# A two-layer retention and attention trunk in float32: the retention heads issued in another order, kept tiles reloaded by GpSimd, weight sums moved by 192 bytes

## The chip, the core and the metric

The kernel runs on one core of one Trainium2 chip. The metric is the device time of one execution in microseconds (us), given as the median of several runs. The profile is of one execution; its times are counted from the start of the span. Engines in the profile: PE is TensorE (PEld its weight loads), DVE is VectorE, ACT is ScalarE, POOL is GpSimd, SP is SyncE. SP does nothing but issue DMAs, and here GpSimd does little else.

## The reference

Two layers, 512 tokens, model width 1024, everything float32. A layer is a half-step SwiGLU FFN, a token mixer, another half-step FFN and a gated per-layer embedding, with an RMS norm ahead of each; the mixer of layer 0 is retention, that of layer 1 is forgetting attention. Each FFN is `h = h + 0.5 * swiglu(rmsnorm(h), w_in, w_out)` with 2816 hidden features. The part that the change touches most is retention, four heads with 256 features for q and k and 512 for v:

```python
def retention(h, w_in, gn_w, w_out):
    q, k, v, g = jnp.split(h @ w_in, ...)
    q = rotary(q); k = rotary(k) * DK ** -0.5
    # per head, causal, with a decay gamma ** (i - j) between tokens i >= j
    s = (q @ k.T) * decay
    o = rmsnorm(s @ v, gn_w)        # per head
    y = silu(g) * o
    return y @ w_out
```

The reference works in chunks of 128 tokens and carries a state. The kernel computes the same as one causal product over the 512 tokens.

## The kernel before, in words

**Products.** A float32 product is made of three TensorE products of rounded halves (`mm3`, L339 to L341): every operand is split into a high part `hi` (a rounding copy, `nc.scalar.copy`, on ScalarE: L329) and a low part `lo` (the operand minus `hi`, on VectorE: L330). Activations live as pairs of 128x512 tiles in four pools, `unit_a` to `unit_d`. Weights come through `Weights`: SP loads a raw tile (L80), ScalarE and VectorE split it (L88, L89); where `negated` is used, ScalarE writes the high part and the negated raw tile (L134, L135) and GpSimd adds the source on top with an accumulating DMA (L136). For the first two heads of retention all output weights (`ret_o`) take this second way.

**Strassen.** The FFNs' input products and retention's projections of q, k and gates are computed in pairs with seven half-size products instead of eight (`Strassen`, its products in `product`, L540). They need sums of weight blocks, `s12`, `s34` and the split block `a12`, which `emit_sums_now` makes on VectorE (L168) and splits, in a pool that is opened per stage (`ffn0` to `ffn3`, and `rsum` for retention). A product of L540 has 128x128 weights from such a tile, and a half-width unit tile (128x256) as the moving operand. By the compiled program's addresses, all unit tiles start at 32 modulo 512 bytes; `s12`, `s34` and `a12` start at 224 modulo 512 in the FFN stages and at 288 in retention; raw weight splits `w8` start at 32 or at 224.

**Retention's stage.** First all projections: v (L525), then 14 Strassen pairs for q, k and gates of the heads. q and k are rotated, gates go through silu, and everything that head 0 doesn't need at once is written to 28 tiles in DRAM (`kept`) by GpSimd DMAs (L798, L824). Then the heads, one after the other:

- `loaded(hd)` reloads q, k and v of a head: eight DMAs of 256 KB into unit tiles (only the four of v for head 0; L832, issued by SP), each followed by a rounding copy on ScalarE (L833) and a subtraction on VectorE (L834).
- `scores(hd)` multiplies q by k (PE), scales by the decay (L889, VectorE) and splits the result into `uhi0..3` and `ulo0..3`; these are the u of the change's title.
- `attended` multiplies u by v into four banks and squares them (L910).
- `head_scale` sums the squares over tokens (L353), `on_rows` brings the scale to rows (L490 transposes, L929).
- `kept_gates(hd)` reloads the gates (`sg`, L945, SP); for head 0 they are computed late (`gate`, L937).
- `outputs(hd)` scales the four banks (L952), multiplies by the gates (L956) and splits into `unit_a` tiles, d = 0 to 3.
- `out_blocks` multiplies former outputs by `ret_o`, one block of 128 output features at a time, and adds to the residual `hall` (L971).

**What sets the order.** TensorE runs the program in the order in which it is written (`manual_schedule`). ScalarE, VectorE, GpSimd and SP are ordered by the scheduler that compiles the kernel, which starts from the program's text and from `issue_after`, which keeps an instruction behind another. Each engine then works strictly in that order: an instruction that waits holds up all that stand behind it on its engine. A DMA that GpSimd issues stands in GpSimd's DMA queue, one that SP issues in another.

**FFN.** `ffn` runs the first two or three hidden blocks plainly (`plain`), because the norm's scale isn't there yet, and the rest as Strassen pairs: `begin` starts a pair's products, `rest` does the others, `next_sums` lets VectorE make the sums of the next. The `columns` and `rows` of the norm bring the scale to token columns and rows between the plain products.

Of the kernel before, what the change touches and what calls it, by code (L numbers as in the profile page):

```python
# [38 lines left out]
class Pair:  # L39
# [3 lines left out]
    def __init__(self, ffn, q, r):  # L43
        self.ffn, self.q, self.r, self.direct = ffn, q, r, False
# [13 lines left out]
class Weights:  # L58
# [3 lines left out]
    def __init__(self, tc, raw_pool, pool):  # L62
        self.tc, self.nc, self.raw_pool, self.pool = tc, tc.nc, raw_pool, pool
        self.plan, self.ready, self.used = [], [], 0
        self.low = self.nc.vector
        self.limit, self.spare = None, []
        self.look, self.placed, self.by_dma, self.by_vector = LOOKAHEAD, {}, set(), set()
        self.shift, self.cast = 0, None
        self.sum_pool, self.open_ffn, self.pairs_used = None, None, 0
        self.ahead, self.behind = 0, ()  # L70
# [87 lines left out]
    def emit_sums_now(self):  # L158
        nc = self.nc
        pairs = [p for p in self.plan[: len(self.ready)] if isinstance(p, Pair) and p.ffn == self.open_ffn]  # L160
        for pair in pairs[: self.pairs_used + self.ahead]:
# [15 lines left out]
            add(s4, s2, a12)  # L177
            add(s3, a21, a11)
            self.split(s4, pair.s[3][:, 0, :], pair.s[3][:, 1, :])
            self.split(s3, pair.s[2][:, 0, :], pair.s[2][:, 1, :])  # L180
            self.negated(a12, pair.x[:, 0, :], pair.x[:, 1, :], pair.r[:, 0:512])
# [20 lines left out]
    def next_sums(self, behind):  # L202
        self.pairs_used += 1
        self.behind = (behind,)
        self.emit_sums()
        self.behind = ()
# [3 lines left out]
def trunk(ctx, tc, a):  # L210
# [24 lines left out]
    for i in range(4):  # L235
        ins = [Pair(i, a["ffn_w_in"][i, m, 0], a["ffn_w_in"][i, m, 1]) for m in range(NF)]
        chunks = CHUNKS[i]
        outs = [[a["ffn_w_out"][i, m][:, k0 * P : k1 * P] for m in range(KB)] for k0, k1 in chunks]
        for m in [PLAIN[i]] + [k1 + 1 for _, k1 in chunks[:-1]]:
            ins[m].direct = ins[m + 1].direct = True  # L240
        ffn_src.append((ins, outs))
# [350 lines left out]
    def ffn(i, n, nxt, stack, apool, meanwhile=None):  # L592
# [61 lines left out]
        if i:  # L654
            whole = [plain(0)]
            n.columns()
            W.begin((n.last,) if n.early else ())
# [13 lines left out]
        last = plain(done - 1, {10: scaled})  # L671
# [92 lines left out]
    def open_retention():  # L764
# [4 lines left out]
        W.open(4, sums.enter_context(tc.tile_pool(name="rsum", bufs=2, reuse_waits="tile")))  # L769
        return stack, hold, sums  # L770

    def retention(n, nxt, pools):
# [53 lines left out]
        def fetched(src, pool=ud):  # L826

            out = []
            for s in range(2):
                hi, lo = new(), unit(pool)  # L830
                raw = lo.bitcast(F32)
                nc.sync.dma_start(out=raw, in_=src[:, s, :])  # L832
# [46 lines left out]
        def scores(hd, q, kk):  # L879
            dk, u = dks.pop(0), []  # L880
            for j in range(NT):
# [13 lines left out]
                split(t1[:, :w], hi, lo)  # L895
# [3 lines left out]
            return u  # L899
# [49 lines left out]
        def outputs(hd, os, sg, rn, y):  # L949
            for d in range(4):  # L950
# [25 lines left out]
        u = scores(0, got["q", 0], got["k", 0])  # L976
# [6 lines left out]
        rn = on_rows(rn)  # L983
        sg.append(gate(3))
        outputs(0, os, sg, rn, y[0])
        u = scores(1, q, kk)
        os, acc = attended(v, u)
        q, kk, v = loaded(2)
        sg = kept_gates(1)
        out_blocks(0, y[0], range(0, 3))  # L990
        rn = head_scale(acc)
        out_blocks(0, y[0], range(3, 5))
        rn = on_rows(rn)
        outputs(1, os, sg, rn, y[1])
        out_blocks(0, y[0], range(5, 8))
        u = scores(2, q, kk)
        os, acc = attended(v, u)
        q, kk, v = loaded(3)
        sg = kept_gates(2)
        out_blocks(1, y[1], range(0, 3))  # L1000
        rn = head_scale(acc)
        out_blocks(1, y[1], range(3, 5))
        rn = on_rows(rn)
        outputs(2, os, sg, rn, y[2])
        out_blocks(1, y[1], range(5, 6))
        u = scores(3, q, kk)
        os, acc = attended(v, u)
# [8 lines left out]
        outputs(3, os, sg, rn, y[3])  # L1016
# [8 lines left out]
    def forgetting(n, nxt):  # L1025
        H = 64
        with tc.tile_pool(name="fox", bufs=1, reuse_waits="tile") as pool:
# [70 lines left out]
            def k_part(p):  # L1098
# [7 lines left out]
                for e in range(2):  # L1106
                    kh = pool.tile([P, S], F32R, name=f"khi{e}")
                    with tc.issue_after(W.cast.ins) if W.cast and e else nullcontext():
# [444 lines left out]
```

## Time and profile before

| | |
|---|---|
| median of 3 runs | 2155.02 us (2150.18, 2155.02, 2155.34) |
| time of the profiled execution | 2150.43 us |
| its span | 2148.4 us |
| PE busy | 2112.7 us (98%) |
| DVE, ACT, POOL busy | 73%, 59%, 12% |
| mean granted TensorE clock | 0.993 |

So the profiled execution has 2.0 us around its span, and stands 4.6 us below the median. Stages by time in the span: FFN 0 to about 370, retention's projections 370 to 577, retention's heads 577 to 735, the second FFN and the embedding to 1157, the third FFN to 1490, attention to 1715, the last FFN to 2080 and the rest to the end.

How to read it: PE is busy nearly all the time, so time is won either where PE sits idle (35.7 us of the span, spread over two dozen places), where its clock is lowered, or where its products are shorter. The list of what PE waits for gives the first, the table of time windows with the column PEclk the second, the list of one line's instructions by operand the third.

### The profile page before, as it was taken

To read this page: it belongs to the slowest core of one execution; us is meant where nothing else is said; L and a number is where in the kernel's file an instruction comes from. 1 tells how busy PE (TensorE), PEld (TensorE's weight loads), DVE (VectorE), ACT (ScalarE), POOL (GpSimd) and SP (SyncE) were. 2 spreads that over 40 slices of the span, in tenths; PEclk is the share of its full clock that TensorE was granted. 3 is DMA by queue.
4 is the path that set the end of the run, shared out by engine and by line. 5 is a ranking of instruction groups with operands and counts; after the bars stand their busy time and mean duration, and the time that the engine had idled before them with its cause. 6 is when DMAs were issued, how large, how long until landed. Compare 5 with 4: busy or idle time off the path is not lost.

```text
span 2148.4 us, 36202 instructions
## 1 busy us (share of the span) xinstructions
PE 2112.7 (98%) x14137; PEld 1940.2 (90%) x14137; DVE 1577.7 (73%) x2920; ACT 1277.7 (59%) x2195; POOL 262.5 (12%) x277
## 2 busy tenths in 40 slices
PE   9999999999989999999999999999999999999997
PEld 9899998999977898999989999998788899999987
DVE  9786868677757687868768787776775687867775
ACT  8474657545655474746557565464786775655655
POOL 0010100121200000101001011010233300100100
PEclk9999999999999999999999999999999999999999
DMA  6475654666756244746526565563412234665631
GB/s 196 116 177 136 160 139 134 172 192 179 228 172 167 79 130 123 175 128 163 146 88 157 125 175 148 138 162 99 127 60 99 98 98 124 172 153 143 158 108 40
DMA packets 106652, 299.96 MB, mean 140 GB/s; under 512 B 11105, under 2 KB 14689, under 8 KB 106481
## 3 DMA queue, kind: packets, MB, share of 16 engines
q1 hardware_dynamic: 69088, 220.26, 30.9%
q0 software_dynamic: 36160, 76.30, 19.7%
q8 instruction: 110, 1.80, 0.3%
q10 hardware_dynamic: 1232, 1.09, 0.2%
q14 instruction: 62, 0.50, 0.1%
HBM read 285.00 MB, written 12.62 MB: 139 GB/s over the span
## 4 chain that ended last, share of the span: by engine, by line
PE 89%; DVE 6%; ACT 3%; DMA 1%; issue 1%; SPq 0%; DVEq 0%; ACTq 0%
PE bank L540 42%; PE bank L339 12%; PE bank L340 12%; PE bank L341 11%; PE bank L617 3%; PE bank L818 1%; PE bank L819 1%; PE bank L820 1%; PE bank L525 1%; PE bank L754 1%; PE bank L756 1%; DVE w L89 1%; PE bank L755 1%; DVE acc L463 1%; DMA wraw<-in_ffn_w_in 1%
## 5 line engine op out<-in xcount | busy, mean ns | idle before, releaser
L88 ACT CAST w<-wraw 128x1024 fp32r<-128x1024 f32 (+1 forms) x207 | 209.6, 1018 | 313.3 <-PE bank L341 203.7
L540 PE MATMUL bank<-unit_a,s 128*128 128x256 f32 x2202 | 325.1, 277 | 0.0
L88 ACT CAST s<-sums 128x512 fp32r<-128x512 f32 x372 | 219.5, 617 | 173.1 <-PE bank L540 85.0
L89 DVE TENSOR_TENSOR s<-sums,s 128x512 fp32r<-128x512 f32 x372 | 246.2, 686 | 102.7 <-ACT s L88 101.8
L540 PEld LDWEIGHTS bank<-unit_a,s 128*128 128x128 f32 x2202 | 287.0, 188 | 0.0
L340 PE MATMUL bank<-unit_d,w 128*128 128x512 f32 x656 | 255.5, 389 | 0.8 <-DVE unit_d L330 0.8
L339 PE MATMUL bank<-unit_d,w 128*128 128x512 f32 x656 | 255.7, 390 | 0.3 <-DVE tmp L1210 0.3
L341 PE MATMUL bank<-unit_d,w 128*128 128x512 f32 x656 | 255.3, 389 | 0.0
L89 DVE TENSOR_TENSOR w<-wraw,w 128x1024 fp32r<-128x1024 f32 (+1 forms) x186 | 218.1, 1173 | 45.4 <-ACT w L88 45.0
L540 PE MATMUL bank<-unit_b,s 128*128 128x256 f32 x1040 | 221.5, 277 | 0.0
L339 PE MATMUL bank<-unit_a,w 128*128 128x512 f32 (+1 forms) x536 | 200.0, 373 | 0.9 <-DVE unit_b L333 0.6
L340 PE MATMUL bank<-unit_a,w 128*128 128x512 f32 (+1 forms) x536 | 198.6, 370 | 0.0
L341 PE MATMUL bank<-unit_a,w 128*128 128x512 f32 (+1 forms) x536 | 198.5, 370 | 0.0
L646 DVE SCALAR_TENSOR_TENSOR tmp<-bank,rows 128x512 f32<-128x512 f32 x96 | 66.1, 689 | 145.2 <-PE bank L341 145.0
L540 PEld LDWEIGHTS bank<-unit_b,s 128*128 128x128 f32 x1040 | 166.0, 189 | 0.0
L540 PE MATMUL bank<-unit_b,w 128*128 128x256 f32 x837 | 153.4, 281 | 0.0
L540 PE MATMUL bank<-unit_a,w 128*128 128x256 f32 x978 | 149.7, 278 | 1.5 <-ACT tmp L568 1.5
L136 POOL DMA_DIRECT2D a<-in_ffn_w_in x80 | 70.2, 877 | 660.8 <-ACT a L135 460.8
L540 PE MATMUL bank<-unit_c,s 128*128 128x256 f32 x682 | 150.0, 277 | 0.0
L340 PEld LDWEIGHTS bank<-unit_d,w 128*128 128x128 f32 x656 | 123.1, 188 | 26.4 <-DVE unit_d L330 1.2
L339 PEld LDWEIGHTS bank<-unit_d,w 128*128 128x128 f32 x656 | 123.1, 188 | 26.1 <-DVE tmp L1210 0.5
L341 PEld LDWEIGHTS bank<-unit_d,w 128*128 128x128 f32 x656 | 123.1, 188 | 25.6
(333 smaller groups left out, 4819.9 us busy)
## 6 DMA issues: line engine op xcount, KB each, us to landing
wraw<-in_ffn_w_in SPq DMA_DIRECT2D x174, 512.0 KB, 4.3
wraw<-in_ffn_w_out SPq DMA_DIRECT2D x64, 512.0 KB, 4.5
w<-in_ffn_w_in POOLq DMA_DIRECT2D x57, 512.0 KB, 5.6
a<-in_ffn_w_in POOLq DMA_DIRECT2D x79, 256.0 KB, 5.9
wraw<-in_ret_p SPq DMA_DIRECT2D x28, 512.0 KB, 3.7
wraw<-in_ffn_w_out SPq DMA_DIRECT2D x32, 384.0 KB, 3.7
kept<-tmp POOLq DMA_DIRECT2D x40, 256.0 KB, 3.7
wraw<-in_ret_v SPq DMA_DIRECT2D x16, 512.0 KB, 4.7
```

The source lines that it names most:

```text
L88: self.cast = self.nc.scalar.copy(hi, raw)
L89: low.tensor_tensor(out=lo, in0=raw, in1=hi.bitcast(F32), op=ALU.subtract)
L136: self.nc.gpsimd.dma_start(out=lo, in_=src, accum_op=ALU.add)
L339: nc.tensor.matmul(out, wh, xh, start=first, stop=False)
L340: nc.tensor.matmul(out, wh, xl, start=False, stop=False)
L341: nc.tensor.matmul(out, wl, xh, start=False, stop=last)
L463: nc.vector.tensor_tensor(out=self.acc[:, ts_], in0=self.acc[:, ts_], in1=sq, op=ALU.add)
L525: nc.tensor.matmul(o[:, half], w[:, ks], x, start=k == t == q == 0, stop=k == KB - 1 and q == 2, skip_group_check=True,)
L540: add = lambda w, x, start, stop: nc.tensor.matmul(out, w, x, start=start, stop=stop, skip_group_check=True)
L617: nc.tensor.matmul(o[:, HALVES[t]], x[:, ks], y, start=k == t == q == 0, stop=k == KB - 1 and q == 2, skip_group_check=True,)
L646: nc.vector.scalar_tensor_tensor(out=t1, in0=o, scalar=-0.5, in1=n.r, op0=ALU.mult, op1=ALU.mult)
L754: nc.tensor.matmul(os[t], xh, wh[:, js], start=k == 0, stop=False)
```

## The change

Six things are changed.

1. The pool `rsum` gets a tile of 48 floats, `apart`, ahead of the others, so that its tiles lie 192 bytes higher.
2. `fetched` issues the reloads of kept tiles from GpSimd instead of SP.
3. The heads are issued in another order. `scores` also hands back its last split. Of the outputs of the former head, d = 0 to 2 (0 and 1 for head 2) are issued ahead of the scores and the rest behind the scores' last split, as are the next head's reloads. The blocks of `out_blocks` are grouped 2, 2, 4 instead of 3, 2, 3, and 2, 2, 2 instead of 3, 2, 1.
4. In the first FFN the pair of hidden block 6 is marked `late`: two of its four sums, their splits and that of `a12` are issued by the following `next_sums`, behind the addition that ends the `begin` there.
5. In the other three FFNs `columns` and the first sums are issued inside the last plain block, behind its third step, and no longer ahead of it.
6. In the attention a rounding copy is kept behind the last weight split only for parts after the first two.

```diff
@@ Pair
-        self.ffn, self.q, self.r, self.direct = ffn, q, r, False
+        self.ffn, self.q, self.r, self.direct, self.late = ffn, q, r, False, False
@@ Weights.emit_sums_now
             self.split(s2, pair.s[1][:, 0, :], pair.s[1][:, 1, :])
-            add(s4, s2, a12)
-            add(s3, a21, a11)
-            self.split(s4, pair.s[3][:, 0, :], pair.s[3][:, 1, :])
-            self.split(s3, pair.s[2][:, 0, :], pair.s[2][:, 1, :])
-            self.negated(a12, pair.x[:, 0, :], pair.x[:, 1, :], pair.r[:, 0:512])
+
+            def later(pair=pair, a11=a11, a12=a12, a21=a21, s2=s2, s3=s3, s4=s4, add=add):
+                add(s4, s2, a12)
+                add(s3, a21, a11)
+                self.split(s4, pair.s[3][:, 0, :], pair.s[3][:, 1, :])
+                self.split(s3, pair.s[2][:, 0, :], pair.s[2][:, 1, :])
+                self.negated(a12, pair.x[:, 0, :], pair.x[:, 1, :], pair.r[:, 0:512])
+
+            if pair.late:
+                self.held = later
+            else:
+                later()
@@ Weights.next_sums
         self.pairs_used += 1
+        if self.held:
+            with self.tc.issue_after(behind.ins):
+                self.held()
+            self.held = None
@@ trunk
+        ins[chunks[0][1]].late = i == 0
@@ ffn
             whole = [plain(0)]
-            n.columns()
-            W.begin((n.last,) if n.early else ())
...
-        last = plain(done - 1, {10: scaled})
+        def summed():
+            n.columns()
+            W.begin((n.last,) if n.early else ())
+
+        last = plain(done - 1, {3: summed, 10: scaled} if i else {10: scaled})
@@ open_retention
-        W.open(4, sums.enter_context(tc.tile_pool(name="rsum", bufs=2, reuse_waits="tile")))
+        rsum = sums.enter_context(tc.tile_pool(name="rsum", bufs=2, reuse_waits="tile"))
+        rsum.tile([P, 48], F32, name="apart", bufs=1)
+        W.open(4, rsum)
@@ fetched
-                nc.sync.dma_start(out=raw, in_=src[:, s, :])
+                nc.gpsimd.dma_start(out=raw, in_=src[:, s, :])
@@ scores
-                split(t1[:, :w], hi, lo)
+                last = split(t1[:, :w], hi, lo)
                 u.append((hi, lo))
             if hd < 2:
                 decay(hd + 2)
-            return u
+            return u, last
+
+        @contextmanager
+        def behind(last):
+            with tc.issue_after(last[0].ins), tc.issue_after(last[1].ins):
+                yield
@@ outputs
-        def outputs(hd, os, sg, rn, y):
-            for d in range(4):
+        def outputs(hd, os, sg, rn, y, ds):
+            for d in ds:
@@ retention, the heads
+        outputs(0, os, sg, rn, y[0], range(3))
         sg.append(gate(3))
-        outputs(0, os, sg, rn, y[0])
-        u = scores(1, q, kk)
-        os, acc = attended(v, u)
-        q, kk, v = loaded(2)
-        sg = kept_gates(1)
-        out_blocks(0, y[0], range(0, 3))
-        rn = head_scale(acc)
-        out_blocks(0, y[0], range(3, 5))
-        rn = on_rows(rn)
-        outputs(1, os, sg, rn, y[1])
-        out_blocks(0, y[0], range(5, 8))
...
-        u = scores(3, q, kk)
-        os, acc = attended(v, u)
+        for hd in (1, 2, 3):
+            u, last = scores(hd, q, kk)
+            with behind(last):
+                outputs(hd - 1, os, sg, rn, y[hd - 1], range(2 if hd == 3 else 3, 4))
+            os, acc = attended(v, u)
+            if hd < 3:
+                with behind(last):
+                    q, kk, v = loaded(hd + 1)
+                sg = kept_gates(hd)
+                out_blocks(hd - 1, y[hd - 1], range(0, 2))
+                rn = head_scale(acc)
+                out_blocks(hd - 1, y[hd - 1], range(2, 4))
+                rn = on_rows(rn)
+                outputs(hd, os, sg, rn, y[hd], range(3 if hd == 1 else 2))
+                out_blocks(hd - 1, y[hd - 1], range(4, 8 if hd == 1 else 6))
@@ forgetting, k part
-                    with tc.issue_after(W.cast.ins) if W.cast and e else nullcontext():
+                    with tc.issue_after(W.cast.ins) if W.cast and e and p > 1 else nullcontext():
```

The changed file is 12 to 21 lines longer ahead of these places: L329, L330, L566, L832, L833, L889, L945, L956 and L971 of before are L341, L342, L578, L848, L849, L905, L966, L977 and L992 there.

**ScalarE at the scores of head 1.** Before (names: `unit_a` are the outputs of head 0, `unit_d_6918` the last v tile of head 1, `unit_d_7273` and `unit_d_7278` the q of head 2):

```order
L937 ACTIVATE sg_7122<-tmp_7120 128x512
L135 ACTIVATE w8_7323<-wraw_7321 128x1024
L329 CAST unit_a_7127<-tmp_7124 128x512
L833 CAST unit_d_6918<-unit_d_6919 128x512
L329 CAST unit_a_7134<-tmp_7131 128x512
L329 CAST unit_a_7141<-tmp_7138 128x512
L833 CAST unit_d_7273<-unit_d_7274 128x512
L329 CAST unit_a_7148<-tmp_7145 128x512
L329 CAST uhi0_7161<-tmp_7159 128x512
L833 CAST unit_d_7278<-unit_d_7279 128x512
L329 CAST uhi1_7174<-tmp_7172 128x384
```

With the change:

```order
L341 CAST unit_a_7069<-tmp_7066 128x512
L134 CAST w8_7324<-wraw_7322 128x1024
L849 CAST unit_d_6914<-unit_d_6915 128x512
L341 CAST unit_a_7076<-tmp_7073 128x512
L135 ACTIVATE w8_7324<-wraw_7322 128x1024
L341 CAST unit_a_7083<-tmp_7080 128x512
L849 CAST unit_d_6919<-unit_d_6920 128x512
L958 ACTIVATE sg_7144<-tmp_7142 128x512
L341 CAST uhi0_7155<-tmp_7153 128x512
L341 CAST uhi1_7168<-tmp_7166 128x384
L341 CAST uhi2_7181<-tmp_7179 128x256
L341 CAST uhi3_7194<-tmp_7192 128x128
```

The copy of the head's own last v tile still stands ahead of `uhi0`; the copies of the next head's q no longer do, and the four copies of u stand together.

**The reloads' queue at the same place.** SP before, from the raw weights of the third block of `ret_o` on (`kept11` holds the last v of head 1, `kept18` and `kept19` its gates, `kept2` the q of head 2):

```order
L832 DMA unit_d_6914<-kept11_4155 128x512
L80 DMA wraw_7476<-in_ret_o 128x1024
L832 DMA unit_d_6919<-kept11_4155 128x512
L945 DMA sg_7313<-kept18_4162 128x512
L945 DMA sg_7315<-kept18_4162 128x512
L945 DMA sg_7317<-kept19_4163 128x512
L832 DMA unit_d_7274<-kept2_4146 128x512
L945 DMA sg_7319<-kept19_4163 128x512
```

GpSimd with the change:

```order
L136 DMA w8_7002<-in_ret_o 128x1024
L848 DMA unit_d_6915<-kept11_4156 128x512
L136 DMA w8_7089<-in_ret_o 128x1024
L848 DMA unit_d_6920<-kept11_4156 128x512
L136 DMA w8_7324<-in_ret_o 128x1024
L848 DMA unit_d_7275<-kept2_4147 128x512
L848 DMA unit_d_7280<-kept2_4147 128x512
```

The reloads left SP's queue, where they stood among raw weights and gates, and now stand between the accumulating DMAs of the weights in GpSimd's.

**VectorE ahead of the scores of head 3.** Before (`unit_a` are the outputs of head 2, of which the four are split here):

```order
L952 SCALAR_TENSOR_TENSOR tmp_7810<-bank_7565,small_93,rnrows_7782 128x512
L330 TENSOR_TENSOR unit_a_7793<-tmp_7789,unit_a_7792 128x512
L956 TENSOR_TENSOR tmp_7803<-tmp_7803,sg_7673 128x512
L330 TENSOR_TENSOR unit_a_7800<-tmp_7796,unit_a_7799 128x512
L956 TENSOR_TENSOR tmp_7810<-tmp_7810,sg_7675 128x512
L330 TENSOR_TENSOR unit_a_7807<-tmp_7803,unit_a_7806 128x512
L971 TENSOR_TENSOR hall_92<-bank_7817,hall_92 128x512
L330 TENSOR_TENSOR unit_a_7814<-tmp_7810,unit_a_7813 128x512
L889 SCALAR_TENSOR_TENSOR tmp_7838<-bank_7831,rk2_4176,acc_7204 128x512
```

With the change (`unit_d_7666` is the head's last v tile):

```order
L973 SCALAR_TENSOR_TENSOR tmp_7771<-bank_7563,small_93,rnrows_7764 128x512
L850 TENSOR_TENSOR unit_d_7666<-unit_d_7666,unit_d_7665 128x512
L977 TENSOR_TENSOR tmp_7771<-tmp_7771,sg_7670 128x512
L973 SCALAR_TENSOR_TENSOR tmp_7778<-bank_7564,small_93,rnrows_7764 128x512
L992 TENSOR_TENSOR hall_92<-bank_7790,hall_92 128x512
L342 TENSOR_TENSOR unit_a_7775<-tmp_7771,unit_a_7774 128x512
L977 TENSOR_TENSOR tmp_7778<-tmp_7778,sg_7672 128x512
L992 TENSOR_TENSOR hall_92<-bank_7804,hall_92 128x512
L905 SCALAR_TENSOR_TENSOR tmp_7825<-bank_7818,rk2_4177,acc_7198 128x512
```

Two of the four outputs moved behind the scaling of the scores, and the last v tile's subtraction moved ahead of it.

More of the change, by code (lines that the diff above doesn't have):

```diff
@@ L1 @@
 import math
-from contextlib import ExitStack, nullcontext
+from contextlib import ExitStack, contextmanager, nullcontext
 import numpy as np
@@ L67, in __init__ @@
         self.look, self.placed, self.by_dma, self.by_vector = LOOKAHEAD, {}, set(), set()
-        self.shift, self.cast = 0, None
+        self.shift, self.cast, self.held = 0, None, None
         self.sum_pool, self.open_ffn, self.pairs_used = None, None, 0
@@ L975, in retention @@
         v = loaded(0)
-        u = scores(0, got["q", 0], got["k", 0])
+        u, _ = scores(0, got["q", 0], got["k", 0])
         sg = [gate(0)]
@@ L983, in retention @@
         rn = on_rows(rn)
+        outputs(0, os, sg, rn, y[0], range(3))
         sg.append(gate(3))
-        outputs(0, os, sg, rn, y[0])
-        u = scores(1, q, kk)
-        os, acc = attended(v, u)
-        q, kk, v = loaded(2)
-        sg = kept_gates(1)
-        out_blocks(0, y[0], range(0, 3))
-        rn = head_scale(acc)
-        out_blocks(0, y[0], range(3, 5))
-        rn = on_rows(rn)
-        outputs(1, os, sg, rn, y[1])
-        out_blocks(0, y[0], range(5, 8))
-        u = scores(2, q, kk)
-        os, acc = attended(v, u)
[L998 to L1005, printed above, removed]
-        u = scores(3, q, kk)
-        os, acc = attended(v, u)
+        for hd in (1, 2, 3):
[13 more added lines that the diff above has]
+                out_blocks(hd - 1, y[hd - 1], range(4, 8 if hd == 1 else 6))
         sg = kept_gates(3)
@@ L1015, in retention @@
         both.first((2, 3))
-        outputs(3, os, sg, rn, y[3])
+        outputs(3, os, sg, rn, y[3], range(4))
         stack.close()
```

## The prediction

> **What bounds the kernel now.** I read the page first, then the list of what PE waits for, then time windows around the largest waits, then PE's commonest line by operand.
>
> ```profile
> PE 2112.7 (98%) x14137; PEld 1940.2 (90%) x14137; DVE 1577.7 (73%) x2920; ACT 1277.7 (59%) x2195; POOL 262.5 (12%) x277
> ```
>
> TensorE is the bound: of the span of 2148.4 us it is idle for 35.7. A change can take that idle time, the time at a lowered clock, or make products shorter. These are the waits that the edits touch (us in total, times, longest):
>
> ```profile
> PE bank L339 <- ACT uhi L329: 13.9, 2, 10.3
> ...
> PE bank L540 <- ACT tmp L568: 1.5, 1, 1.5
> PE bank L353 <- DVE tmp L330: 0.8, 1, 0.8
> ```
>
> The first is the product of u and v: once 10.3 us at head 1, once 3.65 at head 3. Each is followed by a slow clock. In the windows below the columns are PE busy and its count, PEld, DVE, ACT, POOL, then the granted clock, the DMA share and GB/s:
>
> ```profile
> 68.00:73.00 5.00, 3.84 (x32) 3.84 (x33) 3.93 (x8) 3.89 (x8) 0.85 (x1) 1.00 0.70 180
> ...
> 620.00:625.00 5.00, 0.00 (x0) 0.00 (x0) 4.55 (x8) 1.55 (x3) 0.00 (x0) 0.60 1.06 301
> 625.00:630.00 5.00, 3.24 (x7) 2.25 (x8) 3.44 (x8) 2.85 (x6) 0.00 (x0) 0.50 1.03 392
> 630.00:635.00 5.00, 5.00 (x28) 4.57 (x27) 2.40 (x6) 1.64 (x4) 0.00 (x0) 0.88 0.50 177
> ...
> 695.00:700.00 5.00, 2.63 (x5) 1.78 (x6) 5.00 (x10) 1.64 (x4) 0.00 (x0) 0.60 0.00 0
> 700.00:705.00 5.00, 5.00 (x20) 4.34 (x19) 0.51 (x2) 0.00 (x0) 0.00 (x0) 0.71 0.32 105
> ```
>
> At head 1 PE works at half clock from 626.75 to 630 and at 0.88 in the next window: 3.25 x 0.5 + 5 x 0.12 = 2.2 us lost. At head 3, from 697.30: 2.7 x 0.5 + 5 x 0.29 = 2.8. So head 1 costs 12.5 us in all, head 3 6.4.
>
> **Term 1, the 192 bytes: 5.5 us.** The first two rows are retention's projections (370 to 578), the next the second FFN, both L540 by operand (ns least/median/most); the last two are from the chain of waits (start, us, products).
>
> ```profile
> L540 PE MATMUL bank<-unit_a,s x378: 283/283/284, 371.9 to 575.1; 128*128 128x256 f32 x189
> ...
> L540 PE MATMUL bank<-unit_a,w x210: 276/276/283, 370.5 to 572.2; 128*128 128x256 f32 x105
> ...
> L540 PE MATMUL bank<-unit_d,s x540: 276/276/278, 785.6 to 1050.4; 128*128 128x256 f32 x180
> ...
> 521.15 55.67 PE bank L540 x468
> ...
> 859.09 76.80 PE bank L540 x672
> ```
>
> The same product takes 283 ns with retention's sums and 276 with the FFN's, while retention's own raw weights (`unit_a,w`) take 276: it is not the stage. I put the compiled program's addresses beside all 7812 products of this line. Where the weights start 192 bytes beyond the moving operand, modulo 512, they take 276 ns; where they start 0 or 256 beyond, 283, but for a few per cent that differ by 1 to 5 ns. Retention's sums stand 256 beyond now and 448 with the change. The pattern seen repeats every 256 bytes, and 448 is 192 beyond that, so I take 276. Price: the chain gives 55.67/468 = 0.1190 us for one product in retention and 76.80/672 = 0.1143 in the FFN; 14 pairs of 84 products are 1176, and 1176 x 0.0047 = 5.5 us. The bounds are 0 and 5.5; a loss is excluded, as no start differs more than 283. It lies on the path: PE has no idle time there, and no other engine is full.
>
> **Term 2, head 1: 6.5 us.** What holds PE there (ScalarE and PE in order of time):
>
> ```profile
> 619.80 0.62 ACT L833 CAST unit_d<-unit_d 128x512 fp32r<-128x512 f32 x1 [3.22 <-DMA unit_d<-kept]
> ...
> 625.04 0.62 ACT L833 CAST unit_d<-unit_d 128x512 fp32r<-128x512 f32 x1 [2.04 <-DMA unit_d<-kept]
> 626.08 0.61 ACT L329 CAST uhi<-tmp 128x512 fp32r<-128x512 f32 x1
> 626.75 0.79 PE L339 MATMUL bank<-uhi,unit_d 128*128 128x512 f32 x1 [10.29 <-ACT uhi L329]
> ```
>
> ScalarE waits in its queue for two reloads: head 1's last v, then head 2's q. With the change the second stands behind the copies of u, which takes away the 625.04. The first stays ahead, and its DMA now stands in GpSimd's queue, right behind the accumulating DMA of L136 that is issued at 611.26. The rows that price it (issue, and us to landing):
>
> ```profile
> 611.26 0.87 POOL L136 DMA_DIRECT2D w<-in_ret_o  x1 [6.20 <-ACT w L135]
> 612.04 1.64 SPq L945 DMA_DIRECT2D sg<-kept  x3
> w<-in_ret_o POOLq DMA_DIRECT2D x1, 512.0 KB, 6.0
> w<-in_ret_o POOLq DMA_DIRECT2D x1, 512.0 KB, 8.7
> unit_d<-kept SPq DMA_DIRECT2D x1, 256.0 KB, 8.1
> ```
>
> The 6.0 is that of the DMA issued at 604.17, alone; the 8.7 that of 611.26, beside three gate loads and reloads; the 8.1 that of the v reload issued at 611.63, which landed at 619.73. A plain DMA behind an accumulating one on GpSimd's queue is seen in the projections:
>
> ```profile
> 419.97 1.12 POOL L136 DMA_DIRECT2D w<-in_ret_p  x1 [1.61 <-ACT w L135]
> 420.72 0.96 POOL L824 DMA_DIRECT2D kept<-tmp  x1
> w<-in_ret_p POOLq DMA_DIRECT2D x1, 512.0 KB, 7.8
> kept<-tmp POOLq DMA_DIRECT2D x1, 256.0 KB, 8.0
> ```
>
> They land at 427.8 and 428.7: 0.9 us behind. So the reload lands between 611.3 + 6.0 + 0.9 = 618.2 and 611.3 + 8.7 + 0.9 = 620.9. The gate loads now come behind the scores, so I take 618.9, near the free end. Two instructions of ScalarE (0.52 apart above) and 0.67 from u's copy to PE follow: PE starts at 620.6, and is ready at 616.5. That leaves 4.1 us idle (3.4 to 6.1). The clock fell after 3.65 us of idleness and not after the 1.5 in the first FFN, so it probably falls: 2 us of the 2.2 to 2.8. Gain 12.5 - 6.1 = 6.4, say 6.5, with 3.9 and 9 as ends.
>
> The Trainium skill (TensorE: Matmul & The Clock Gate, Part 1) says that the clock halves after at least one idle window of about 3.4 us that runs freely. By that rule a stall of 4.1 us holds a whole window only now and then, and the time would come out 2 us lower; the trace does not quite agree: 0.60 in the window 695 to 700 is one microsecond at full and four at half, so the clock fell at 696.0, 2.4 us after PE had stopped at 693.65.
>
> The Trainium skill (DMA: Bandwidth & Descriptors, Queues, rings and completion order) says that a DMA engine takes turns between the queue rows it has work for, packet by packet. By that rule a reload on SP shares with the accumulation from the start and, being half its size, lands ahead of it instead of 0.9 us behind: it speaks against this part of the change, and with the reloads left on SP the forecast would be at least 0.9 us lower. The trace agrees that the GpSimd pair above landed one behind the other; no row shows the SP case without the gate loads.
>
> **Head 2: -0.3 us.** Its reloads stand among two accumulations, and one block less lies between the squares and the sums over tokens. Before, at head 2 (the first two rows are one block apart):
>
> ```profile
> 671.90 0.44 PE L339 MATMUL bank<-unit_a,w 128*128 128x512 f32 x1
> ...
> 674.71 0.39 PE L339 MATMUL bank<-unit_a,w 128*128 128x512 f32 x1
> 677.17 0.69 DVE L330 TENSOR_TENSOR tmp<-tmp 128x512 fp32r<-128x512 f32 x1
> 680.15 0.95 PE L353 MATMUL bank<-ones_r,tmp 128*128 128x2 f32 x8
> ```
>
> A block is 2.8 us, and the cover is 680.15 - 677.86 = 2.3 us, so half a microsecond is missing. The squares stood behind reloads' copies there, which move away, so about a microsecond comes back; that leaves -0.5 to +0.5 for each of two heads, and up to 1.3 more if a late reload holds VectorE. I take -0.3, bounds -2 and +0.3.
>
> **Term 3, head 3: 5 us.** VectorE is the late one:
>
> ```profile
> 689.73 0.39 PE L339 MATMUL bank<-unit_d 128*128 128x512 f32 x1
> ...
> 695.85 1.66 DVE L889 SCALAR_TENSOR_TENSOR tmp<-bank,rk,acc 128x512 f32<-128x512 f32 x3
> 696.63 1.34 ACT L329 CAST uhi<-tmp 128x512 fp32r<-128x512 f32 x3 [1.84 <-DVE tmp L889]
> 697.30 0.79 PE L339 MATMUL bank<-uhi,unit_d 128*128 128x512 f32 x1 [3.65 <-ACT uhi L329]
> ```
>
> PE had the scores at 693.65, VectorE reached them at 695.85, being full (5.00 of 5 in the window). Two of four outputs go behind, six instructions of some 0.6 us: 3.7 us less ahead. But the sums over tokens come 2.8 us earlier, and the last v reload, on GpSimd behind an accumulation, holds VectorE's queue with its subtraction. Counted from the transposes to rows (L490): PE has those (0.4 us), two blocks (5.6) and the scores (693.65 - 689.73 = 3.9) and is ready at 9.9. By the order the accumulation is issued some 3 us ahead of the transposes, so the reload lands at 6.0 + 0.9 - 3 = 3.9 (3.3 to 4.6), its copy ends 0.6 later, and eleven instructions of 0.6 us lead to `ulo0`: 10.5 to 11.8, 11.1 in the middle. That is 0.6 to 1.9 us of idleness, of which I take 1.4, at full clock. Gain 6.4 - 1.4 = 5.0 (4.5 to 5.8).
>
> **Terms 4 and 5, the FFNs: 1.5 and 0.8 us.** In the first FFN:
>
> ```profile
> 67.78 0.43 DVE L566 TENSOR_TENSOR bank<-bank,tmp 128x256 f32<-128x256 f32 x1
> 68.75 0.35 ACT L568 COPY tmp<-bank 128x256 f32<-128x256 f32 x1
> 69.16 0.51 PE L540 MATMUL bank<-unit_a,w 128*128 128x256 f32 x2 [1.50 <-ACT tmp L568]
> ```
>
> Ahead of L566 stood sums and splits of weights of some 0.6 us each; by the order five of them now stand behind it. The 1.5 us go (0.7 at least). In the other FFNs `columns` runs later, behind 18 products of the last plain block; the 0.8 us wait of the list goes, but the chain to the rows has about 5 us left for some 4, so -1 to +0.8. The condition in the attention moves no instruction: 0.
>
> **Sum.** 5.5 + 6.5 - 0.3 + 5 + 1.5 + 0.8 = 19 us off the profiled 2150.4: 2131.4. That execution is with the lowest of the runs shown, and the median stands 4.6 above it. I put the median of the new runs at 2132.
>
> **Rivals.**
> - The accumulation lands late and head 1 keeps its whole stall: the v reload at 623 instead of 618.9, with gate loads still beside it. For it: 8.7 us where DMA is full. Against: the gates are issued later now. Idle 623 + 1.7 - 616.5 = 8.2 and 2.2 of clock leave a gain of 2.1 there instead of 6.5: 2136.5.
> - The bytes have no effect, because 448 is not 192: 2132 + 5.5 = 2137.5. For it: no sum tile stands at 448. Against: 276 and 283 depend on nothing else.
> - The reload is quick, head 1 idles 2 us or less and the clock holds: 4 us better, 2128.
> - Slower: GpSimd's queue is strictly in order, and its accumulations wait for ScalarE and for free tiles. If each reload waits for two accumulations instead of one (8.7 us more), heads 2 and 3 idle some 9.5 us and lose 2.5 to the clock, 12 each: 2150.4 - 7.8 + 12 + (12 - 6.4) = 2160. It decides from the second accumulation ahead of a head's last reload on. The order shows one at each, so this is unlikely.
> - The first two together, with stalls at head 2: 2146.
>
> **How the numbers follow.** Forecast 0.5, late accumulation 0.18, no effect of the bytes 0.1, quick reload 0.14, slower 0.03, the mixture 0.05. The range, 2121 to 2144, takes the high ends (5.5 + 9 + 0.3 + 5.8 + 1.5 + 0.8, with the quick reload) and the low ones with the median's 4.6 on top. A measurement of this kernel can tell about 0.3%, 6.5 us: faster by more than that 0.92, within it 0.05, slower 0.03.
>
> **What would show it.** L540 at 276 ns for `s` between 370 and 578, the stage 5.5 us shorter; a wait for `uhi` of some 4 us at head 1 with ScalarE's copy of the v tile right ahead, some 1.4 at head 3 without a clock drop; no wait at L568 near 69 us nor at L353 near 1163. I am wrong if L540 stays at 283 ns, if PE waits over 7 us at a head, or if L353 or L490 show waits of over 2 us in the heads.

## The result

The changed kernel takes 2133.36 us (median of 4 runs, 2132.34 to 2134.32), the kernel before 2153.28 (4 runs, 2150.18 to 2155.34): a ratio of 0.9909, 95% interval 0.9891 to 0.9926. It is faster by 0.9%, and 2132 had been predicted. The profiled execution took 2132.34 us with a span of 2130.4, so the span is 18.0 us shorter than before. The page's line of engines and, of the list of what PE waits for, the waits that the prediction spoke of:

```profile
span 2130.4 us, 36214 instructions
PE 2103.9 (99%) x14137; PEld 1932.5 (91%) x14137; DVE 1576.7 (74%) x2920; ACT 1277.8 (60%) x2195; POOL 279.0 (13%) x305
PE bank L351 <- ACT uhi L341: 6.0, 2, 5.3
...
PE bank L365 <- DVE tmp L342: 0.5, 1, 0.5
...
PE bank L552 <- DMA w<-in_ret_p: 0.2, 1, 0.2
```

The waits for `uhi` fell from 13.9 us to 6.0, the wait at L568 in the first FFN (now L580) is gone, and two new ones are there: 0.5 for the sums over tokens of head 2 (L365; 0.65 with a second, shorter one) and one for the accumulating DMA of retention's weights. PE's busy time fell by 8.8 us, which is shorter products and less half clock. In both traces PE runs its 14137 products in nearly the same order, so the start of one and the same product in the two gives what each stage contributed:

| stage | predicted | measured |
|---|---|---|
| first FFN | -1.5 | -2.0 |
| retention's projections | -5.5 | -4.5 |
| head 1 (scores to the end of attended) | -6.5 | -5.1 (24.17 to 19.09) |
| head 2 (from there to its end) | +0.3 | -0.5 (35.21 to 34.68) |
| head 3 (the same) | -5.0 | -3.8 (35.89 to 32.06) |
| third and fourth FFN | -0.8 | -1.0 and -0.5 |
| attention | 0 | -0.6 |
| sum | -19 | -18.0 |

The products of the projections by operand (ns least, median, most) are the ones foreseen:

```profile
L552 PE MATMUL bank<-unit_a,s x378: 276/276/280, 369.9 to 568.7; 128*128 128x256 f32 x189
...
L552 PE MATMUL bank<-unit_a,a x83: 276/276/280, 381.8 to 569.9; 128*128 128x256 f32 x83
```

At head 1, ScalarE's copy of the last v tile stands right ahead of `uhi`, and its DMA took 8.1 us (issues on GpSimd, their landing times, then ScalarE and PE):

```profile
604.67 0.86 POOL L136 DMA_DIRECT2D w<-in_ret_o  x1 [0.24 <-ACT w L135]
605.31 0.78 POOL L848 DMA_DIRECT2D unit_d<-kept  x1
w<-in_ret_o POOLq DMA_DIRECT2D x1, 512.0 KB, 8.1
unit_d<-kept POOLq DMA_DIRECT2D x1, 256.0 KB, 8.1
613.42 0.62 ACT L849 CAST unit_d<-unit_d 128x512 fp32r<-128x512 f32 x1 [3.69 <-DMA unit_d<-kept]
613.94 0.62 ACT L958 ACTIVATE sg<-tmp 128x512 f32<-128x512 f32 x1
614.47 0.60 ACT L341 CAST uhi<-tmp 128x512 fp32r<-128x512 f32 x1
615.13 0.79 PE L351 MATMUL bank<-uhi,unit_d 128*128 128x512 f32 x1 [5.25 <-ACT uhi L341]
```

The windows show the clock falling there, and holding at head 3, where PE idled 0.70 and 0.58 us:

```profile
610.00:615.00 5.00, 0.00 (x0) 0.00 (x0) 2.05 (x4) 1.58 (x3) 2.55 (x5) 0.76 1.02 283
615.00:620.00 5.00, 4.85 (x12) 3.50 (x13) 3.46 (x9) 1.91 (x5) 0.00 (x0) 0.55 1.06 341
...
680.00:685.00 5.00, 3.71 (x23) 3.17 (x22) 5.00 (x10) 2.48 (x5) 0.00 (x0) 1.00 0.00 0
683.23 0.49 PE L351 MATMUL bank<-uhi,unit_d 128*128 128x512 f32 x1 [0.70 <-ACT uhi L341]
...
684.31 0.50 PE L352 MATMUL bank<-ulo,unit_d 128*128 128x512 f32 x1 [0.58 <-DVE ulo L342]
```

### The profile page after: what moved, and what is told of

It is laid out like the page before. It is cut to its first block, busy times and chain, and to the rows that moved or that the text cites. A ratio compares the mean times of both kernels' runs of the same rounds, so it can differ in the third digit from the quotient of the medians.

```text
span 2130.4 us, 36214 instructions
## 1 busy us (share of the span) xinstructions
PE 2103.9 (99%) x14137; PEld 1932.5 (91%) x14137; DVE 1576.7 (74%) x2920; ACT 1277.8 (60%) x2195; POOL 279.0 (13%) x305
## 4 chain that ended last, share of the span: by engine, by line
PE 86%; DVE 4%; issue 4%; ACT 2%; DMA 2%; POOL 1%; SPq 0%; POOLq 0%; DVEq 0%; ACTq 0%
PE bank L552 41%; PE bank L351 12%; PE bank L352 11%; PE bank L353 11%; PE bank L629 4%; DMA w<-in_ret_p 1%; DMA unit_d<-kept 1%; PE bank L768 1%; PE bank L835 1%; PE bank L836 1%; PE bank L834 1%; PE bank L769 1%; PE bank L770 1%; DMA wraw<-in_ffn_w_in 1%; DVE w L89 1%
```

## The experiments

Three questions were open. Is it the 192 bytes, and are they worth 5 us by themselves? What makes head 1's v reload land 8.1 us after its issue, the place in GpSimd's queue or what else the DMA engines do? And which of the edits carries the gain?

**The bytes alone.** The kernel before with only this:

```diff
-        W.open(4, sums.enter_context(tc.tile_pool(name="rsum", bufs=2, reuse_waits="tile")))
+        rsum = sums.enter_context(tc.tile_pool(name="rsum", bufs=2, reuse_waits="tile"))
+        rsum.tile([P, 48], F32, name="apart", bufs=1)
+        W.open(4, rsum)
```

> The kernel before with one thing changed: the pool of retention's weight sums starts 192 bytes higher. Theory (address): the products with s and a operands in retention's projections take 276 ns instead of 283, and the projections get 5.3 us shorter, less the waits of some 0.8 us for the accumulating DMAs of the weights that showed up with the whole change; the rest of the kernel stays, so 4.5 to 5.5 us in all, 0.2 to 0.3%. Rival (the shorter products came from the other reloads and orders, not from the address): 283 ns stay, and the time is that of the kernel before.

Measured: 2149.14 us against 2150.87, ratio 0.9986 (0.9977 to 0.9996). The products, a wait at head 0's sums over tokens, what held ScalarE ahead of them, and the window behind:

```profile
L540 PE MATMUL bank<-unit_a,s x378: 276/276/280, 371.8 to 572.1; 128*128 128x256 f32 x189
...
PE bank L353 <- ACT tmp L329: 1.4, 1, 1.4
...
593.50 0.62 ACT L835 CAST unit_d<-unit_d 128x512 fp32r<-128x512 f32 x1 [4.06 <-DMA unit_d<-kept]
...
600.00:602.50 2.50, 2.50 (x14) 2.50 (x13) 0.67 (x4) 2.47 (x4) 0.00 (x0) 0.50 0.00 0
```

The products are short, as the theory has it, and the projections end 3.1 us earlier (a wait of 1.5 us at 427 us for an accumulating DMA of the weights takes most of the rest). But PE then reaches the sums of head 0 before the squares are there: a copy of a reload for head 1 stands ahead of them on ScalarE and waits 4.06 us for its data. PE idles 1.87 us in all, the clock halves, and at 609 us the kernel is 0.6 us later than before; in this profile 0.3 us of the span is left. The address theory holds, and the time expected from it doesn't.

**Another shift.** The same with 64 floats:

```diff
+        rsum.tile([P, 64], F32, name="apart", bufs=1)
```

> The kernel before with the pool of retention's sums 256 bytes higher, so that its tiles start 0 beyond the moving operand modulo 512 instead of 256. Theory (the pattern repeats every 256 bytes): 283 ns stay in retention's projections, 120 ns from start to start, no gain. Rival (288 modulo 512 alone is bad, or any shift helps): 276 ns and 5 us less in the projections.

Measured, one run: 2150.48 us, and in retention's projections

```profile
L540 PE MATMUL bank<-unit_a,s x378: 283/283/283, 371.8 to 575.0; 128*128 128x256 f32 x189
```

So a shift as such does nothing: 0 and 256 bytes beyond the moving operand are slow, 192 and 448 fast.

**The whole change without the bytes.**

> The changed kernel without the 192 bytes. Theory (bytes alone gained 3 us in the projections and lost them again at head 0, where a reload stood ahead of the squares of head 0 on ScalarE; with the new order nothing late stands there, so what the projections win is kept): 4 to 5 us above the changed kernel, 2137 to 2139. Rival (the time after the projections is set by the reloads whatever PE does before): less than 1.5 us above it.

Measured: 2138.2 us (ratio to before 0.9944, 0.9929 to 0.9959), 4.8 above the changed kernel; the same product is 4.5 us later at the end of the projections and still 4.5 later at the end of the heads. So here the 192 bytes keep their gain. The reason expected for it, that nothing late stands ahead of head 0's squares, holds, but the order isn't what brings it. In the changed kernel copies of reloads stand there too, and they come in time:

```profile
584.75 1.64 ACT L849 CAST unit_d<-unit_d 128x512 fp32r<-128x512 f32 x3
586.55 2.07 ACT L931 ACTIVATE tmp<-bank 128x512 f32<-128x512 f32 x4 [0.15 <-PE bank L353]
```

The changed kernel with the reloads back on SP (below) has the same order, and there one of them is late again: it is the move to GpSimd that frees head 0.

**The move to GpSimd alone.** The kernel before with

```diff
-                nc.sync.dma_start(out=raw, in_=src[:, s, :])
+                nc.gpsimd.dma_start(out=raw, in_=src[:, s, :])
```

> The kernel before with the 28 reloads issued by GpSimd and nothing else changed. Theory (the queue of GpSimd puts a reload behind the accumulating DMA ahead of it): head 1's last v lands about 8 us after its issue, as on SP before, and head 2's q still stands ahead of the copies of u on ScalarE, so head 1 idles 8 to 11 us instead of 10.3, and heads 2 and 3 lose up to 2 us each by reloads behind accumulations: minus 1 to plus 6 us against the kernel before. Rival (the move itself frees the queue of SP and is what wins at the heads): 5 to 9 us less in the heads.

Measured: 2152.99 us against 2150.87, ratio 1.0006 (0.9997 to 1.0015). Its list has

```profile
PE bank L339 <- ACT uhi L329: 15.8, 2, 11.1
```

instead of 13.9: the queue alone wins nothing in time.

**The changed kernel with the reloads back on SP** (the reverse of that diff):

> The changed kernel with the 28 reloads back on SP. Theory (a reload on SP shares the DMA engines with the accumulation from the start instead of following it, as the Trainium skill has it in DMA: Bandwidth & Descriptors, Queues, rings and completion order): head 1's last v lands 4 to 6 us after its issue instead of 8.1, PE idles 2 to 4 us there instead of 5.25, and the time is 1 to 4 us below the changed kernel. Rival (raw weights and gates in SP's queue come in the way, so that GpSimd is the better place): head 1 idles 6 us or more and the clock falls as well, 1 to 8 us above the changed kernel.

Measured: 2134.42 us, ratio to before 0.9921 (0.9907 to 0.9936), which can't be told from the changed kernel. First head 0's copy of a reload, ahead of the squares; then head 1's reload with its landing and that of the accumulation issued at 606.55, and the copy that waits for the reload:

```profile
588.14 0.62 ACT L849 CAST unit_d<-unit_d 128x512 fp32r<-128x512 f32 x1 [3.89 <-DMA unit_d<-kept]
...
606.92 0.32 SPq L848 DMA_DIRECT2D unit_d<-kept  x1
w<-in_ret_o POOLq DMA_DIRECT2D x1, 512.0 KB, 8.6
unit_d<-kept SPq DMA_DIRECT2D x1, 256.0 KB, 8.0
...
614.91 0.62 ACT L849 CAST unit_d<-unit_d 128x512 fp32r<-128x512 f32 x1 [3.29 <-DMA unit_d<-kept]
...
PE bank L351 <- ACT uhi L341: 5.9, 1, 5.9
```

The reload took 8.0 us on SP, beside the accumulation, and 8.1 on GpSimd, behind it: the theory misses, and the queue makes no difference in this pair. By the rule of the Trainium skill (DMA: Bandwidth & Descriptors, Queues, rings and completion order) that a DMA engine takes turns between its queue rows, the SP reload was to land ahead of the accumulation; the trace agrees, but only by 0.2 us (614.9 and 615.1), and the accumulation took longer as well (8.6 us, not 8.1). The rival comes near at head 1 (5.9 us of idleness against 6 or more), but a time above the changed kernel isn't shown.

The other parts balance. The projections are 1.1 us shorter, all of it at 475 and 527 us, where two accumulating DMAs of the weights held PE in the changed kernel and don't here; why these landed sooner isn't shown. The late reload ahead of head 0's squares costs 3, and head 3 is 1.9 shorter.

**No accumulation ahead of the reload.** The changed kernel, with one of head 0's output weight tiles split by ScalarE and VectorE:

```diff
-        W.by_dma |= {id(x) for hd in (0, 1) for x in ret_o[hd]}
+        W.by_dma |= {id(x) for hd in (0, 1) for x in ret_o[hd]} - {id(ret_o[0][1])}
```

> The changed kernel with the second weight tile of head 0's output split by ScalarE and VectorE instead of by an accumulating DMA, so that no accumulation stands ahead of the reload of head 1's last v. Theory (the reload lands 8.1 us after its issue because it follows the accumulation, which takes that long): it lands in 3 to 5 us, PE idles 0 to 2.5 us at head 1 instead of 5.25, the clock holds, and the time is 4 to 7 us below the changed kernel. Rival (the DMA engines are full with gates, reloads and raw weights, so that the reload takes 7 to 8 us anyway, as it did on SP): within 1.5 us of the changed kernel, and VectorE's added 1.2 us may cost as much.

Measured: 2131.97 us (ratio to before 0.9913, 0.9898 to 0.9928). The reload, and the windows behind it:

```profile
604.82 0.54 POOL L848 DMA_DIRECT2D unit_d<-kept  x1 [0.89 <-PE bank L537]
unit_d<-kept POOLq DMA_DIRECT2D x1, 256.0 KB, 3.3
...
610.00:615.00 5.00, 2.95 (x6) 2.06 (x7) 4.97 (x11) 2.56 (x6) 2.52 (x5) 0.64 0.77 193
615.00:620.00 5.00, 5.00 (x19) 4.32 (x19) 0.23 (x1) 0.00 (x0) 0.54 (x1) 0.68 1.04 327
```

3.3 us instead of 8.1: without the accumulation the reload is fast on the same queue. PE idles 2.7 us instead of 5.25. But VectorE is late next (4.97 of 5 busy), and the clock falls after 2.4 us of idleness and stays down: head 1 gains 1.8 us, where 4 to 7 had been expected. At head 3 PE idles 1.28 us as in the changed kernel, yet here the clock falls and takes 1.6 us. That the accumulation ahead of it makes the reload late on GpSimd's queue is confirmed; the gain is within the rival's bounds.

**Gates out of the way.** The changed kernel with the gate loads issued by ScalarE behind the last split of the scores:

```diff
-                    nc.sync.dma_start(out=s_, in_=x[:, s, :])
+                    (nc.scalar if hd < 3 else nc.sync).dma_start(out=s_, in_=x[:, s, :])
...
+                with behind(last):
-                sg = kept_gates(hd)
+                    sg = kept_gates(hd)
```

> The changed kernel with the gate loads of heads 1 and 2 issued by ScalarE behind the last split of the scores instead of by SP as soon as their tiles are free. Theory (the five gate loads issued at 609.67 share the DMA engines with the accumulation and the reload behind it): the reload lands 1 to 2 us sooner, PE idles 3.3 to 4.3 us at head 1 instead of 5.25, 1 to 4 us below the changed kernel. Rival (the accumulation alone sets it): the reload lands 8 us after its issue as before, within 1 us of the changed kernel.

Measured: 2135.72 us (ratio 0.9927, 0.9911 to 0.9944), with

```profile
606.87 0.78 POOL L848 DMA_DIRECT2D unit_d<-kept  x1
...
614.81 0.62 ACT L849 CAST unit_d<-unit_d 128x512 fp32r<-128x512 f32 x1 [2.95 <-DMA unit_d<-kept]
```

7.9 us: as long as the accumulation is ahead of it, the gates don't matter to the landing. There the rival holds; the time is 2.4 us above the changed kernel by the medians, with waits of 1.4 us in the projections and 2.7 around head 2's sums in this execution.

**The FFN and attention edits alone**, on the kernel before:

> The kernel before with the edits outside retention alone: the late sums of the first FFN, the later columns and sums of the other FFNs, and the condition in the attention. Theory (they act where they stand): 2.0 us less in the first FFN, 1.0 in the third, 0.5 in the fourth, 0.6 or nothing in the attention, of which the 2.0 is lost again at the heads as with the bytes alone: 1.5 to 4 us less in all. Rival (the gains belong to the bytes and the order): under 1 us in all.

Measured: 2146.34 us against 2150.32, ratio 0.9981 (0.9972 to 0.999). The same products start 1.8 us earlier after the first FFN, 1.0 more after the third and 0.5 more after the fourth; of the 1.8, 0.6 is lost by the end of the heads. The 0.6 that the table has for the attention is no proof for its edit, because the next kernel, without that edit, gains 1.7 there between 1540 and 1645 us.

**The order of the heads alone**, on the kernel before, reloads on SP:

> The kernel before with the new order of the heads alone: reloads on SP, no 192 bytes, the FFNs and the attention as before. Theory (the order frees the copies of u from head 2's q and takes VectorE's outputs out of head 3's way; the queue makes no difference to head 1's reload): head 1 idles 5 to 6 us instead of 10.3, head 3 under 0.5 instead of 3.65 with the clock held, 8 to 13 us less than the kernel before. Rival (without the move to GpSimd reloads, raw weights and gates in SP's queue eat the gain): less than 5 us less.

Measured: 2142.5 us against 2151.19, ratio 0.9958 (0.9943 to 0.9973): 8.7 us, the largest part of the change. Its profiled execution was its fastest (2138.23), and shows

```profile
PE bank L351 <- ACT uhi L341: 3.2, 1, 3.2
PE bank L365 <- DVE tmp L342: 2.3, 4, 0.9
...
w<-in_ret_o POOLq DMA_DIRECT2D x1, 512.0 KB, 8.6
unit_d<-kept SPq DMA_DIRECT2D x1, 256.0 KB, 5.3
```

one wait for `uhi`, at head 1, instead of two, and waits at the sums of heads 0, 1 and 2 (0.45, 0.66 and 1.03 us with those for ScalarE; the longest of the row, 0.9, lies behind the heads). The last two rows are head 1's last v reload, issued by SP at 612.37, and the accumulation issued 0.37 us ahead of it. This reload landed in 5.3 us, 3.0 ahead of the accumulation, where the kernel with the reloads back on SP had 8.0 with the same loads in flight at the same distances. So on SP its landing varies, and one execution of each kernel doesn't show what the queue alone is worth.

The four parts alone multiply to a ratio of 0.9931, against 0.9909 for the whole; the difference lies within what these intervals can tell.

**Towards a better kernel.** First, the kernel without the accumulation, and two outputs of head 0 ahead of the scores of head 1 instead of three:

```diff
-        outputs(0, os, sg, rn, y[0], range(3))
+        outputs(0, os, sg, rn, y[0], range(2))
...
-                outputs(hd - 1, os, sg, rn, y[hd - 1], range(2 if hd == 3 else 3, 4))
+                outputs(hd - 1, os, sg, rn, y[hd - 1], range(3 if hd == 2 else 2, 4))
```

> The changed kernel with the second output weight tile of head 0 split without an accumulating DMA, as in the run before, and with only two of head 0's four outputs ahead of the scores of head 1 instead of three. Theory (with the reload in time VectorE is the late one at head 1, busy with three outputs; one less is 1.9 us): PE idles 0.3 to 1 us at head 1 instead of 2.7, the clock holds, and the time is 4 to 6 us below the changed kernel, about 2128. Rival (the clock falls for the other short stalls, as it did at head 3 in the run before after 1.3 us of idleness): 1 to 3 us below it.

Measured: 2133.91 us (ratio 0.992, 0.9905 to 0.9935), a miss: PE idles 3.9 us at head 1, where the reload landed only 6.5 us after its issue, beside six gate loads, and 1.33 us of idleness at head 2's sums halve the clock:

```profile
667.50:670.00 2.50, 1.92 (x10) 1.74 (x11) 2.42 (x5) 1.54 (x3) 0.00 (x0) 0.83 0.02 7
670.00:672.50 2.50, 2.50 (x7) 1.93 (x7) 1.44 (x7) 2.18 (x4) 0.84 (x2) 0.50 0.04 13
```

Second, the last weight tile of head 1 split without an accumulation as well, and head 0's v on SP:

```diff
-        W.by_dma |= {id(x) for hd in (0, 1) for x in ret_o[hd]} - {id(ret_o[0][1])}
+        W.by_dma |= {id(x) for hd in (0, 1) for x in ret_o[hd]} - {id(ret_o[0][1]), id(ret_o[1][3])}
...
-                nc.gpsimd.dma_start(out=raw, in_=src[:, s, :])
+                (nc.sync if pool is ua else nc.gpsimd).dma_start(out=raw, in_=src[:, s, :])
```

> As the kernel with two outputs ahead, and also the last output weight tile of head 1 split without an accumulating DMA, so that none stands ahead of the last reload of head 3, and head 0's v reloaded by SP. Theory (VectorE waits 1.6 us at head 3 for that reload, and the four reloads of head 0 ahead of accumulations in GpSimd's queue cost the projections 0.7 us): head 3 idles 0 to 0.5 us instead of 1.3, the projections get 0.5 to 1 us shorter, 1 to 3 us below the kernel with two outputs ahead. Rival (the added subtraction of 1.2 us on VectorE and a reload on SP ahead of head 0's squares take it back): no lower than that kernel.

Measured: 2130.59 us (ratio 0.9904, 0.9887 to 0.992). Head 3 has no idle time left and is 2.5 us shorter than in the changed kernel; the projections are not shorter in this execution (a wait of 1.5 us for an accumulating DMA), and head 1 still idles 4.4 us. What is late there is again a reload, now beside six gate loads:

```profile
604.07 3.73 SPq L966 DMA_DIRECT2D sg<-kept  x6
...
611.47 0.62 ACT L849 CAST unit_d<-unit_d 128x512 fp32r<-128x512 f32 x1 [3.40 <-DMA unit_d<-kept]
```

With its order the scheduler had moved a raw load that used to hold the gates back in SP's queue. So third, head 1's gate loads issued by ScalarE behind the last split, in addition:

> The kernel of the run before with one thing more: the gate loads of head 1 issued by ScalarE behind the last split of head 1's scores. In that run six gate loads left SP at 604.1 to 607.8, because the scheduler had moved a raw weight load that used to hold them, and head 1's v reload, issued at 605.2 with no accumulation ahead of it, landed only at 611.4. Theory (not the accumulation as such but whatever shares the DMA engines in those microseconds sets the landing): with the gates out of the way the reload lands 3 to 4 us after its issue, PE idles 0.3 to 1.5 us at head 1 instead of 4.4, and the time is 4 to 7 us below the changed kernel, 2126 to 2129. Rival (the reload lands late for another reason, or the clock falls after a short stall all the same): 2130 to 2133.

Measured: 2126.12 us (2124.24 to 2127.88), ratio to before 0.988, interval 0.9864 to 0.9897. The reload's landing, what is left of the waits, and the window at head 1:

```profile
unit_d<-kept POOLq DMA_DIRECT2D x1, 256.0 KB, 3.0
...
PE bank L351 <- ACT uhi L341: 1.8, 1, 1.8
...
610.00:615.00 5.00, 3.71 (x9) 2.73 (x10) 4.57 (x10) 2.46 (x6) 2.51 (x4) 0.66 0.82 194
```

All its runs lie below all those of the changed kernel, 7.2 us by the medians and 6.2 by the ratios to before. On GpSimd's queue an accumulation ahead of the reload and gate loads beside it each suffice to make it late (8 and 6 us), and without both it lands in 3.0. PE still idles 2.1 us at head 1, and the clock still falls. The rivals of this step are refuted as to the time, and the one on the clock is right as to the clock.

## Why the prediction came out, and where it didn't

**The bytes** (5.5 us from 14 pairs at 0.0047). The step held: 276 ns at all sums, as the repetition every 256 bytes had it. 4.5 of the 5.3 to 5.5 remained, since PE, being faster, met the accumulating DMAs of the weights (0.8 us of waits). "It lies on the path" was too simple: alone, the win is lost 30 us later in the profiled execution. It counts because the reloads ahead of head 0's squares come in time in the changed kernel, which goes with the move to GpSimd: with the same order and bytes, SP's reloads cost 3 us there. The prediction had added the terms as if they were independent and had seen nothing at head 0.

**Head 1** (6.5 us, from a reload that lands at 618.9 behind an accumulation). Measured 5.1. The landing 0.6 us behind the accumulation was as priced (0.9), the accumulation itself took 8.1 and not 6.7: the term of the sum that was mis-sized. The choice near the free end rested on the gates being away, and the run with late gates shows that this was worth little: there the accumulation took 7.8 us and the reload behind it 7.9. The reason given, a place behind the accumulation in GpSimd's queue, holds: in all eight traces with the reloads on GpSimd a reload issued right behind an accumulation lands behind it, and without the accumulation head 1's lands in 3.3 us. What didn't come is the at least 0.9 us that the reloads were to win on SP: head 1's landed ahead of the accumulation there, but in 8.0 us. The idle time came to 5.25 us instead of 4.1, the lost clock to 2.2 instead of 2.

**Heads 2 and 3** (-0.3 and 5.0, measured 0.5 and 3.8). Together 4.4 of 4.7. The 1.29 us of idleness at head 3 were predicted as 1.4, with the clock holding. The half microsecond that the cover of two blocks was short came at head 2's sums (0.65 us of idleness, counted in the table with head 3), and nowhere else in the changed kernel.

**The FFNs** (1.5 and 0.8). 2.0, 1.0 and 0.5; the fourth FFN's gain had been left out of the value taken, though it lay in the chain that was priced. The attention's 0 stands, as far as the runs can tell.

**The rivals.** The late accumulation came true in part (head 1 gained 5.1 us, between the 6.5 forecast and the rival's 2.1), the bytes without effect and the quick reload didn't come, and the slower case was far off: one accumulation stood ahead of each last reload, as the order showed. The move to GpSimd measures as neutral alone (1.0006) and in the whole change, but not part by part: it won 3 us at head 0 and lost 1.1 in the projections and 1.9 at head 3.

**The clock** ("fell after 3.65 us and not after 1.5") was right at both heads, at head 3 by luck of the place: in the kernel without the accumulation the clock fell after the same 1.28 us. Such a threshold can't be read from two cases.

## What to carry to other kernels

Before time saved ahead of a stage is added to a sum, ask what PE meets next: here 3 us were lost at the first reload that stood ahead of something PE needs, and kept where that reload came in time. A load that an in-order engine waits for is to be issued away from accumulating DMAs and from bursts of loads that nobody waits for; behind an accumulation on the same queue it lands behind it, and another queue is no safe way out, so look at every DMA in flight in those microseconds. Don't count a shortened stall as a clock kept: at head 1 the halved clock cost 2.2 us after 5.25 us of idleness and 3.1 after 2.7 (in the kernel without the accumulation).

## What the hardware showed that was not expected

- The speed of a 128x256 product with 128x128 weights depends on where its operands start: 276 ns where the weights start 192 or 448 bytes beyond the moving operand modulo 512, 283 where they start 0 or 256 beyond (120.0 ns from start to start for the products of retention's sums in the kernel before, 113.4 for those of the FFNs' sums).
- A plain load of 256 KB lands in 3.0 to 3.3 us with no accumulation or gate load beside it (head 1 of two kernels) and in about 6 beside six gate loads. Issued by GpSimd right behind an accumulating DMA of 512 KB, it landed behind that one in all eight traces that have the reloads there, by 0.6 us at the least. Issued by SP 0.4 us behind one, head 1's landed ahead of it in all six traces of that kind, by 0.2 to 3.0 us, which is 5.3 to 8.2 us after its issue.
- The granted clock changes only at points that lie whole multiples of 3.41 us apart within an execution. In the changed kernel it is half from 612.63 to 619.46, two such periods, and from 1530.82 to 1534.23, one, and these begin 269 periods apart. What follows a period goes with PE's idleness inside it: in the fourteen traces every period at full clock with 1.7 us of idleness or more was followed by half clock and none with less than 0.9; from 0.99 to 1.53 both are seen, and what decides there stays open. A stall that straddles two periods counts in each with its part, as the periods around head 2's sums show, in the first kernel with two outputs ahead, where the clock fell, and in the last kernel, where it held:

```profile
665.74:669.15 3.41, 2.08 (x13) 1.50 (x12) 3.22 (x6) 2.33 (x4) 0.00 (x0) 1.00 0.00 0
...
659.38:662.79 3.41, 2.86 (x13) 2.01 (x11) 3.07 (x5) 2.44 (x6) 0.00 (x0) 1.00 0.06 22
662.80:666.20 3.40, 2.64 (x15) 2.29 (x16) 3.32 (x7) 2.24 (x5) 0.00 (x0) 1.00 0.02 5
```

The same 1.3 us of idleness lies in one period in the first and in two in the last. The Trainium skill (TensorE: Matmul & The Clock Gate, Part 1) gives an idle window of about 3.4 us that runs freely. The traces agree on a window that runs freely and on its length, but the clock fell after windows with only 1.0 to 2.4 us of idleness too, and here the measurement decides.
